# An MLP that changes from its first matrix to its second one token group at a time, with sums of squares added on GpSimd

## The chip, the cores and the metric

The kernel runs on one core of a Trainium2 chip. The metric is the device time of one execution in microseconds (us); several executions are timed, and their median counts. Beside them one execution is profiled: the profile shows what each engine did in it. TensorE is called PE in the profile, VectorE DVE, ScalarE ACT, GpSimd POOL and SyncE, which issues the DMAs, SP.

## The reference

Two layers of a streaming encoder for 1056 tokens (a prompt of 1024 and 32 new ones) and a model width of 1024. Layer 0 mixes tokens with forgetting attention, layer 1 with a gated linear recurrence. The change touches what follows each mixer:

```python
x = x + rmsnorm(out, post_mix_norm[layer])
h = rmsnorm(x, pre_ffn_norm[layer])
u = jax.nn.relu(h @ ffn_w_up[layer])                       # 1024 -> 4096
x = x + rmsnorm((u * u) @ ffn_w_down[layer], post_ffn_norm[layer])   # 4096 -> 1024

def rmsnorm(x, g):
    y = xf * lax.rsqrt(jnp.mean(xf * xf, axis=-1, keepdims=True) + EPS)
    return y * g
```

All of it is float32. A norm needs the sum of squares over the 1024 features of a token before any of its results can be used.

## The kernel before

**Layout.** Features lie on the 128 partitions, tokens along the free axis. The tokens are cut into 4 quarters of 264 (`G`); quarters 0 and 2 are group `c = 0`, quarters 1 and 3 group `c = 1`, and a group's two quarters are its halves `h`. A vector operation on one block of 128 features of a group has 128x528 elements.

**Matmuls.** A float32 operand is written as the sum of two rounded parts, hi and lo, and a product is three matmuls (hi·hi, lo·hi, hi·lo). Making the two parts of a weight block is a *cut* (`cut`: ACT writes hi at L397, DVE subtracts it at L398 for lo), of activations a *split* (`split`, L316 and L317). `unit` multiplies a block of weights (256 columns, up to 4 pairs of 128 rows each) with the activations by seven block products instead of eight. For it the activations of a group are stored as seven *forms* (the four blocks and three combinations of them), and the weights need combinations too, which POOL adds into `Sx` (L336). Each product needs one cut, so a unit has seven cuts and four POOL combinations. With `cs = (0, 1)` a unit uses each cut weight for both groups, with `cs = (0,)` for one. `unit8` does the same block with eight plain products for one group and needs only forms 0, 1, 2 and 4.

**The MLP in `tail`.** `up(i)` computes 256 hidden columns (i = 0 to 15), squares their ReLU, and writes their seven forms to DRAM (`uf`, by `put_u`): a *set*. `down(s)` adds up to four sets into one of four column blocks of the result, so its s runs from 0 to 18 and its first and last units have 1, 2 or 3 pairs. `get_forms(p, c)` reads set p of group c back in parts (264 KB or 132 KB each) through the staging tile `st`, which has four slots, and splits each part into one of four `F` tiles per group. These same `F` tiles hold the operand of the up matrix until its last unit is through with them. Group 0 goes through units 14 to 18 first (`down`), then group 1 (`down8`), so that the norm of group 0 runs beside the matmuls of group 1. The weights come by `load` into two buffers in turn.

**The norms.** `postnorm` runs over eight feature blocks of a group. DVE multiplies y by gain and factor (L276), adds it to x (L279); ACT squares x into `st` (L251), and DVE adds that to a running sum (L252, in `square`). After the eighth block PE adds the sums across partitions by a matmul with ones (`sums`, tile `cs`, L219); from it `rsqrt` makes the factor `rr` of the next norm. `postnorm` runs three times in each layer's `tail` with squares or without: for group 0 and for group 1 after the mixer (kind 1), and for both groups after the MLP (kind 3), the latter with squares in layer 0 alone. `next_h` makes the normed operand of layer 1 from layer 0's result: its sum, then eight products (L789), eight hi parts on ACT (L791) and eight lo parts on DVE (L792).

**Order.** The engines' queues are in order. A scheduler places the instructions; code under `soon()` gets precedence, `behind` and `pin` fix where a PE instruction stands. The PE queue waits at each `cs` matmul until the sum is complete.

Of the kernel before, what the change touches and what calls it, by code (L numbers as in the profile page):

```python
# [26 lines left out]
LAG = 14  # L27
# [38 lines left out]
class K:  # L66
    def __init__(self, ctx, tc, io):
# [9 lines left out]
        self.table = self.pinned = None  # L77
# [185 lines left out]
    def postnorm(self, c, y, x, fr, kind, layer, more=True, hs=(0, 1), tmp=None):  # L263
        sl = slice(hs[0], hs[-1] + 1)
        last = None

        def put(ins):
            nonlocal last
            if last is not None and ins is not None:
                self.behind(ins, last)  # L270
            last = ins or last

        todo = {}
        for j in range(NJ + 2):
            if j < NJ:
                put(self.v.scalar_tensor_tensor(out=y[:, j, sl], in0=y[:, j, sl], scalar=self.gcol(kind, layer, j),  # L276
                                                in1=fr[:, sl], op0=ALU.mult, op1=ALU.mult))
            if 1 <= j <= NJ:
                put(self.v.tensor_tensor(x[:, j - 1, sl], x[:, j - 1, sl], y[:, j - 1, sl], op=ALU.add))  # L279
                if more:  # L280
                    todo[j - 1] = self.square(c, x[:, j - 1, sl], j - 1, hs, tmp)
            if j >= 2 and more:
                put(todo[j - 2](self.v))
# [87 lines left out]
    def unit8(self, c, raw, pairs, evac):  # L371
        nk = len(pairs)
        F = self.F[c]
        for m, (x, z) in enumerate((("A", "B"), ("E", "B"))):
            x, z = self.bank(x), self.bank(z)
            for e, (f, g) in enumerate(((0, 1), (2, 4))):
# [10 lines left out]
                if e == 1:  # L387
                    with self.soon():
                        evac(m, e, 1, z)

# [124 lines left out]
    def tail(self, w_out, layer, sc=None):  # L515
# [5 lines left out]
        with ExitStack() as ctx:  # L521
# [9 lines left out]
            def raws(ring):  # L531
# [4 lines left out]
                def load(src):  # L536
                    n[0] += 1
                    r = rw[n[0] % 2][:, 0:src.shape[1], 0:src.shape[2]]
# [137 lines left out]
            for i in range(NA, 16):  # L676
# [8 lines left out]
            def get_forms(p, c, n=4):  # L685
                for a, b in ((0, 2), (2, 4), (4, 6), (6, 7)):
# [65 lines left out]

            nsq, self.nl = [0, 0], 0
            for s in range(LAG):
                for p in range(4) if s == 0 else (s,) if s > 3 else ():
                    for c in range(2):
                        get_forms(p, c)
                down(s, (0, 1), load)
            get_forms(LAG, 1)
            for s in range(LAG, 19):  # L760
                if s < 16:
                    get_forms(s, 0)
                down(s, (0,), load)
# [17 lines left out]
            def next_h(c, late):  # L781
# [5 lines left out]
                for j in range(NJ):  # L787
# [4 lines left out]
                    self.v.tensor_tensor(hl[:, j], y, hh[:, j].bitcast(F32), op=ALU.subtract)  # L792
# [3 lines left out]
            get_forms(15, 1, 2)  # L796
# [5 lines left out]
            else:  # L802
                next_h(0, self.last_mm)
            for s in range(16, 19):
                down8(s, 1, load2)
# [814 lines left out]
```

## Time and profile before

| | |
|---|---|
| median of 3 runs | 3016.42 us (3013.67 to 3016.75) |
| the profiled execution | 3009.45 us, its span 3007.7 us |
| PE busy | 2845.7 us, 95% of the span |
| DVE busy | 2053.5 us, 68% |
| ACT busy | 1472.0 us, 49% |
| POOL busy | 1468.6 us, 49% |
| mean granted PE clock | 0.972 |
| DMA | 349.36 MB, mean 116 GB/s |

Times inside the profile count from the start of the span. PE is busy nearly throughout; a change of the time must come from the stretches in which it waits or runs at a lower clock, or must make new ones.

### The profile page before, as it was taken

How to read it: one execution, taken by the hardware profiler on the slowest of the kernel's cores; microseconds unless marked ns; L12 is line 12 of the kernel's file. 1: busy time of each engine (PE TensorE's matmuls, PEld its weight loads, DVE VectorE, ACT ScalarE, POOL GpSimd, SP SyncE). 2: the span in 40 equal slices, each digit the busy share in tenths (PEclk: the TensorE clock that was granted, in tenths of full speed). 3: DMA queues.
4: the chain of work that ended last, by engine and by line, in shares of the span. 5: the costliest groups of instructions: out<-in, count | busy, mean ns of one | idle time of the engine just before them, and what ended most of it. 6: DMA issues, size and time to landing. Idle time of an engine off the chain costs nothing.

```text
span 3007.7 us, 56032 instructions
## 1 busy us (share of the span) xinstructions
PE 2845.7 (95%) x21377; PEld 2725.1 (91%) x21377; DVE 2053.5 (68%) x3419; ACT 1472.0 (49%) x3104; POOL 1468.6 (49%) x1595
## 2 busy tenths in 40 slices
PE   7999999999889998999979999999988999899987
PEld 6888888899889998999869999999988999799986
DVE  6788888864785545678888655546488554667787
ACT  6455555555455655544454232322345665644443
POOL 2344444431227775466723644544314886556660
PEclk9999999999989999999989999999999999899997
DMA  5111211144434445445353211115444443544452
GB/s 163 47 48 46 55 46 48 52 113 142 137 129 173 158 145 183 153 132 152 111 161 118 57 56 40 48 33 150 145 126 161 154 166 144 192 143 135 148 166 76
DMA packets 329172, 349.36 MB, mean 116 GB/s; under 512 B 19535, under 2 KB 287703, under 8 KB 328903
## 3 DMA queue, kind: packets, MB, share of 16 engines
q1 hardware_dynamic: 327879, 345.65, 36.6%
q8 instruction: 168, 2.75, 0.4%
q14 instruction: 101, 0.83, 0.1%
q0 software_dynamic: 1024, 0.13, 0.0%
HBM read 238.78 MB, written 106.88 MB: 115 GB/s over the span
## 4 chain that ended last, share of the span: by engine, by line
PE 70%; DVE 13%; DMA 5%; ACT 4%; issue 4%; POOL 4%; SPq 0%; DVEq 0%; ACTq 0%; POOLq 0%
PE mA L410 14%; PE mB L410 11%; PE hj L184 8%; PE pj L184 8%; PE mE L410 5%; PE gp L184 4%; PE po L184 4%; DMA st<-uf 2%; DVE S L398 2%; PE mD L410 1%; DVE F L317 1%; PE lv L1465 1%; POOL hs L310 1%; PE pv L1129 1%; PE ss L1002 1%
## 5 line engine op out<-in xcount | busy, mean ns | idle before, releaser
L410 PE MATMUL mA<-F,S 128*128 128x264 f32 x4404 | 604.8, 289 | 50.3 <-ACT F L316 15.5
L410 PEld LDWEIGHTS mA<-F,S 128*128 128x128 f32 x4404 | 566.0, 191 | 62.8 <-ACT F L316 17.2
L410 PE MATMUL mB<-F,S 128*128 128x264 f32 x4248 | 585.5, 287 | 11.1 <-DVE S L398 4.8
L410 PEld LDWEIGHTS mB<-F,S 128*128 128x128 f32 x4248 | 548.4, 191 | 17.5 <-DVE S L398 9.0
L398 DVE TENSOR_TENSOR S<-Sx,S 128x512 fp32r<-128x512 f32 (+3 forms) x280 | 247.6, 889 | 157.3 <-ACT S L397 155.0
L398 DVE TENSOR_TENSOR S<-raw,S 128x512 fp32r<-128x512 f32 (+3 forms) x282 | 240.4, 857 | 89.6 <-ACT S L397 89.5
L317 DVE TENSOR_TENSOR F<-st,F 128x528 fp32r<-128x528 f32 (+2 forms) x260 | 229.1, 885 | 100.0 <-ACT F L316 99.3
L316 ACT CAST F<-st 128x528 fp32r<-128x528 f32 (+2 forms) x260 | 153.6, 596 | 252.4 <-DMA st<-uf 238.6
L410 PE MATMUL mE<-F,S 128*128 128x264 f32 x1740 | 246.4, 289 | 17.9 <-DVE S L398 9.3
L184 PE MATMUL pj<-H,wh 128*128 128x352 f32 x1152 | 256.7, 341 | 2.1 <-POOL wh L163 1.5
L336 POOL TENSOR_TENSOR Sx<-raw 128x512 f32<-128x512 f32 (+3 forms) x140 | 187.9, 1345 | 132.1 <-DVE S L398 129.6
L410 PEld LDWEIGHTS mE<-F,S 128*128 128x128 f32 x1740 | 225.3, 190 | 26.2 <-DVE S L398 14.5
L310 POOL TENSOR_TENSOR hs<-hs 128x264 f32<-128x264 f32 x216 | 188.4, 891 | 103.5 <-ACT hs L549 101.0
L184 PE MATMUL hj<-h,wh 128*128 128x264 f32 x1600 | 228.7, 289 | 0.0
L170 POOL TENSOR_SCALAR wh<-wr 128x1024 fp32r<-128x1024 f32 x58 | 69.0, 1190 | 319.2 <-PE hj L184 100.2
L184 PEld LDWEIGHTS pj<-H,wh 128*128 128x128 f32 x1152 | 199.8, 192 | 19.0 <-POOL wh L163 1.7
L200 POOL TENSOR_TENSOR e<-e,Y 128x264 f32<-128x264 f32 x170 | 164.0, 974 | 102.1 <-ACT e L741 87.3
L171 DVE TENSOR_TENSOR wl<-wr,wh 128x1024 fp32r<-128x1024 f32 x102 | 135.3, 1328 | 111.1 <-POOL wh L170 59.4
L184 PEld LDWEIGHTS hj<-h,wh 128*128 128x128 f32 x1600 | 206.1, 189 | 1.6
L397 ACT CAST S<-Sx 128x512 fp32r<-128x512 f32 (+3 forms) x280 | 163.6, 585 | 51.3 <-PE mE L410 22.1
L397 ACT CAST S<-raw 128x512 fp32r<-128x512 f32 (+3 forms) x282 | 161.3, 574 | 45.4 <-PE mB L410 32.5
L1125 DVE TENSOR_TENSOR pl<-pf,ph 128x512 fp32r<-128x512 f32 x192 | 127.6, 669 | 54.2 <-POOL ph L1124 29.7
(351 smaller groups left out, 5879.0 us busy)
## 6 DMA issues: line engine op xcount, KB each, us to landing
st<-uf SPq DMA_DIRECT2D x192, 264.0 KB
uf<-hs SPq DMA_DIRECT2D x54, 924.0 KB
raw<-in_ffn_w_up_dram SPq DMA_DIRECT2D x40, 1024.0 KB
raw<-in_ffn_w_down_dram SPq DMA_DIRECT2D x30, 1024.0 KB
wr<-in_hgrn_w_in_dram SPq DMA_DIRECT2D x39, 512.0 KB
wr<-in_fox_w_in_dram SPq DMA_DIRECT2D x32, 512.0 KB
uf<-us SPq DMA_DIRECT2D x10, 924.0 KB
st<-uf SPq DMA_DIRECT2D x64, 132.0 KB
```

The source lines that it names most:

```text
L170: self.g.tensor_scalar(out=wh, in0=raw, scalar1=1.0, scalar2=0.0, op0=ALU.mult, op1=ALU.add)
L171: self.v.tensor_tensor(wl, raw, wh.bitcast(F32), op=ALU.subtract)
L184: ins = self.nc.tensor.matmul(ps, lhsT=ws[kk][a], rhs=xs[kk][b], start=i == 0, stop=i == tot - 1)
L200: self.g.tensor_tensor(out, a, b, op=op)
L310: ins = e.tensor_tensor(f[:, o], f[:, a], f[:, b], op=ALU.subtract)
L316: self.s.copy(hi, src)
L317: self.v.tensor_tensor(lo, src, hi.bitcast(F32), op=ALU.subtract)
L336: self.g.tensor_tensor(src, a, b, op=op)
L397: self.s.copy(hi, src)
L398: self.v.tensor_tensor(lo, src, hi.bitcast(F32), op=ALU.subtract)
L410: ins = self.nc.tensor.matmul(o, lhsT=a[:, i], rhs=F[kp % 4][:, b, f], start=start and n == 0, stop=stop and n == tot - 1, skip_group_chec ...
L1125: self.v.tensor_tensor(pl[:, :N], pf[:, :N], ph[:, :N].bitcast(F32), op=ALU.subtract)
```

## The change

Five edits, in both layers unless said otherwise:

1. The adds of squares in `postnorm` go to GpSimd (`self.g`) instead of DVE, and are no longer chained into DVE's order.
2. The last up unit and the first four down units are done for one group at a time. Up 15 runs for group 0, then for group 1; down 0, 1 and 2 follow for group 0, and the rest alternate. Five more units are cut and combined, and five more weight blocks are loaded.
3. Sets 14 and 15 of group 1, which only `unit8` uses, are read as forms 0, 1, 2 and 4: three parts of 2, 1 and 1 forms instead of four parts of 2, 2, 2 and 1.
4. The weights of down unit 18 (2 of 8 rows) go into the upper half of the buffer that holds those of unit 17 (4 of 8 rows).
5. In layer 0 `next_h(0)` is called after the first half of `down8(16)` instead of ahead of it, and its odd lo parts are subtracted on GpSimd.

```diff
@@ postnorm
             if j >= 2 and more:
-                put(todo[j - 2](self.v))
+                todo[j - 2](self.g)
@@ unit8
                 if e == 1:
                     with self.soon():
                         evac(m, e, 1, z)
+                    if m == 0 and self.mid:
+                        f, self.mid = self.mid, None
+                        f(self.last_mm)
@@ raws
-                def load(src):
-                    n[0] += 1
-                    r = rw[n[0] % 2][:, 0:src.shape[1], 0:src.shape[2]]
+                def load(src, at=0):
+                    n[0] += at == 0
+                    r = rw[n[0] % 2][:, at:at + src.shape[1], 0:src.shape[2]]
@@ tail
-            for i in range(NA, 16):
+            for i in range(NA, 15):
...
-            def get_forms(p, c, n=4):
-                for a, b in ((0, 2), (2, 4), (4, 6), (6, 7)):
+            def get_forms(p, c, n=4, parts=((0, 2), (2, 4), (4, 6), (6, 7))):
+                for a, b in parts:
...
-            for s in range(LAG):
-                for p in range(4) if s == 0 else (s,) if s > 3 else ():
-                    for c in range(2):
-                        get_forms(p, c)
+            up(15, (0,), (hst[2],))
+            get_forms(0, 0)
+            get_forms(1, 0)
+            up(15, (1,), (hst[3],))
+            get_forms(2, 0)
+            down(0, (0,), load)
+            get_forms(3, 0)
+            for p in range(4):
+                get_forms(p, 1)
+            for c, s in ((0, 1), (0, 2), (1, 0), (0, 3), (1, 1), (1, 2), (1, 3)):
+                down(s, (c,), load)
+            for s in range(4, LAG):
+                for c in range(2):
+                    get_forms(s, c)
                 down(s, (0, 1), load)
-            get_forms(LAG, 1)
+            few = ((0, 2), (2, 3), (4, 5))
+            get_forms(LAG, 1, parts=few)
             for s in range(LAG, 19):
                 if s < 16:
                     get_forms(s, 0)
-                down(s, (0,), load)
+                down(s, (0,), load if s < 18 else lambda src: load(src, 4))
...
-                    self.v.tensor_tensor(hl[:, j], y, hh[:, j].bitcast(F32), op=ALU.subtract)
+                    (self.g if j % 2 else self.v).tensor_tensor(hl[:, j], y, hh[:, j].bitcast(F32), op=ALU.subtract)
...
-            get_forms(15, 1, 2)
+            get_forms(15, 1, 2, few)
...
             else:
-                next_h(0, self.last_mm)
+                self.mid = lambda late: next_h(0, late)
             for s in range(16, 19):
-                down8(s, 1, load2)
+                down8(s, 1, load2 if s < 18 else lambda src: load2(src, 4))
```

What the edits move on DVE is seen at two places, and on PE at a third. The first is DVE's queue in layer 0's `postnorm` of group 0 after the attention (`ya` is the mixer's result, `xa` the residual, `wl` the lo part of a weight block of the output projection that PE works on meanwhile). Before, with the adds of squares `st` in line:

```order
L279 TENSOR_TENSOR xa_867_8886<-xa_867_8886,ya_866_8885 128x528
L252 TENSOR_TENSOR st_8881<-st_8881 128x528
L276 SCALAR_TENSOR_TENSOR ya_866_8885<-ya_866_8885,gain,rr_9430 128x528
L279 TENSOR_TENSOR xa_867_8886<-xa_867_8886,ya_866_8885 128x528
L171 TENSOR_TENSOR wl_9663<-wr_9660,wh_9662 128x1024
L252 TENSOR_TENSOR st_8881<-st_8881 128x528
L276 SCALAR_TENSOR_TENSOR ya_866_8885<-ya_866_8885,gain,rr_9430 128x528
```

The same place in the changed program:

```order
L279 TENSOR_TENSOR xa_867_8886<-xa_867_8886,ya_866_8885 128x528
L276 SCALAR_TENSOR_TENSOR ya_866_8885<-ya_866_8885,gain,rr_9430 128x528
L171 TENSOR_TENSOR wl_9663<-wr_9660,wh_9662 128x1024
L279 TENSOR_TENSOR xa_867_8886<-xa_867_8886,ya_866_8885 128x528
L276 SCALAR_TENSOR_TENSOR ya_866_8885<-ya_866_8885,gain,rr_9430 128x528
L279 TENSOR_TENSOR xa_867_8886<-xa_867_8886,ya_866_8885 128x528 x2
```

All seven adds of this `postnorm` are gone from DVE's queue; the other rows keep their order but for one `wl`, which moves ahead of an `xa` add.

The second place is DVE's queue at the start of the down matrix in layer 0 (`F` the splits of sets read back, `S` the cuts, whose size tells the unit: 128x128 is down 0, 128x256 down 1; `Y` the result). Before:

```order
L317 TENSOR_TENSOR F_919_9752<-st_8881,F_919_9752 128x528
L724 TENSOR_TENSOR Y_1200_13956<-mB_14071,e_14101 128x264
L398 TENSOR_TENSOR S_9964<-Sx_9965,S_9964 128x128
L317 TENSOR_TENSOR F_920_9761<-st_8881,F_920_9761 128x528
L398 TENSOR_TENSOR S_9964<-raw_934_9962,S_9964 128x256
L317 TENSOR_TENSOR F_919_9752<-st_8881,F_919_9752 128x264
L317 TENSOR_TENSOR F_978_10693<-st_8881,F_978_10693 128x528
L317 TENSOR_TENSOR F_977_10684<-st_8881,F_977_10684 128x528
```

In the changed program, down 0 of group 0 and the first cuts of down 1:

```order
L401 TENSOR_TENSOR S_9964<-Sx_9965,S_9964 128x128 x2
L401 TENSOR_TENSOR S_9964<-raw_934_9962,S_9964 128x128
L728 TENSOR_TENSOR Y_1184_13719<-mB_14025,e_14044 128x264
L401 TENSOR_TENSOR S_9964<-Sx_9965,S_9964 128x128
L317 TENSOR_TENSOR F_921_9770<-st_8881,F_921_9770 128x528
L401 TENSOR_TENSOR S_9964<-raw_935_9963,S_9964 128x256 x2
L317 TENSOR_TENSOR F_976_10675<-st_8881,F_976_10675 128x528
L728 TENSOR_TENSOR Y_1184_13719<-mB_14063,e_14058 128x264
```

Before, splits of both groups (`F_918` to `F_921` are group 0, `F_976` to `F_979` group 1) stand between few cuts; in the changed program each unit of one group brings its own seven cuts, and from the first cut of up 15 to the first cut of down 4 there are 70 cuts instead of 35, with the same splits.

The third place is PE's queue at the sum of squares that `next_h(0)` needs in layer 0 (`cs`; `mA`, `mE` are result banks). Before:

```order
L410 MATMUL mE_18075<-F_978_10693,S_9964 128x264
L410 MATMUL mE_18075<-F_979_10702,S_9964 128x264
L219 MATMUL cs_17983<-st_8881,ones 128x264
L219 MATMUL cs_17991<-st_8881,ones 128x264
L410 MATMUL mA_18026<-F_977_10684,S_9964 128x264
```

In the changed program:

```order
L413 MATMUL mA_18214<-F_978_10693,S_9964 128x264
L413 MATMUL mA_18214<-F_979_10702,S_9964 128x264
L219 MATMUL cs_18122<-st_8881,ones 128x264
L219 MATMUL cs_18130<-st_8881,ones 128x264
L413 MATMUL mE_18164<-F_977_10684,S_9964 128x264
```

Between the sum ahead of it (for the norm after the MLP) and this one PE has 117 matmuls before and 138 in the changed program.

## Rows read from the trace of the kernel before

**Rows 1.** The page's busy time of each engine (us, share, instructions).
```profile
PE 2845.7 (95%) x21377; PEld 2725.1 (91%) x21377; DVE 2053.5 (68%) x3419; ACT 1472.0 (49%) x3104; POOL 1468.6 (49%) x1595
```

**Rows 2.** Timeline of PE: sums that it waited for; idle time in brackets.
```profile
799.51 1.16 PE L219 MATMUL cs<-st,ones 128*128 128x264 f32 x4 [1.35 <-DVE st L252]
868.25 2.12 PE L219 MATMUL cs<-st,ones 128*128 128x264 f32 x4 [5.58 <-DVE st L252]
1553.36 2.13 PE L219 MATMUL cs<-st,ones 128*128 128x264 f32 x4 [6.78 <-DVE st L252]
1611.82 1.75 PE L219 MATMUL cs<-st,ones 128*128 128x264 f32 x4 [3.29 <-DVE st L252]
2210.67 2.13 PE L219 MATMUL cs<-st,ones 128*128 128x264 f32 x4 [3.51 <-DVE st L252]
2279.65 2.13 PE L219 MATMUL cs<-st,ones 128*128 128x264 f32 x4 [8.01 <-DVE st L252]
```

**Rows 3.** Timeline of PE in layer 0's change of matrix.
```profile
1164.14 3.09 PE L410 MATMUL mA<-F,S 128*128 128x264 f32 x24
1203.11 1.03 PE L410 MATMUL mA<-F,S 128*128 128x264 f32 x3 [7.48 <-ACT Y L712]
1236.40 3.10 PE L410 MATMUL mA<-F,S 128*128 128x264 f32 x24
```

**Rows 4.** Busy time by stretch: PE, PEld, DVE, ACT, POOL; clock, DMA share, GB/s.
```profile
779.00:800.00 21.00, 19.65 (x162) 19.40 (x161) 20.31 (x28) 9.59 (x18) 3.90 (x2) 1.00 0.45 142
849.00:869.00 20.00, 14.42 (x113) 13.97 (x112) 19.16 (x30) 10.93 (x22) 2.46 (x4) 0.89 0.54 187
1164.00:1257.00 93.00, 78.68 (x592) 76.09 (x591) 62.26 (x103) 53.53 (x125) 41.96 (x45) 0.91 0.57 186
1462.00:1500.00 38.00, 32.96 (x239) 30.90 (x237) 34.52 (x45) 19.55 (x42) 29.40 (x26) 0.96 0.25 77
1526.00:1554.00 28.00, 17.14 (x123) 15.99 (x122) 26.02 (x46) 14.30 (x27) 1.55 (x2) 0.82 0.27 89
1554.00:1586.00 32.00, 24.84 (x165) 22.63 (x164) 28.34 (x52) 17.14 (x36) 8.48 (x8) 0.93 0.28 78
```

**Rows 5.** Timeline of DVE in layer 0's first postnorm: start, duration.
```profile
784.52 0.70 DVE L279 TENSOR_TENSOR xa<-xa,ya 128x528 f32<-128x528 f32 x1
785.13 0.70 DVE L252 TENSOR_TENSOR st<-st 128x528 f32<-128x528 f32 x1
785.75 0.76 DVE L276 SCALAR_TENSOR_TENSOR ya<-ya,gain,rr 128x528 f32<-128x528 f32 x1
```

**Rows 6.** Timeline of POOL just after it: adds of other squares.
```profile
801.09 2.75 POOL L252 TENSOR_TENSOR st<-st 128x528 f32<-128x528 f32 x2 [6.66 <-ACT st L251]
805.90 1.39 POOL L252 TENSOR_TENSOR st<-st 128x528 f32<-128x528 f32 x1 [2.05 <-DVE st L252]
```

**Rows 7.** Timeline of DVE beside those adds.
```profile
802.09 0.43 DVE L209 SCALAR_TENSOR_TENSOR rt<-cs,rr 128x264 f32<-128x264 f32 x1 [0.91 <-ACT rr L207]
802.56 1.57 DVE L210 SCALAR_TENSOR_TENSOR rt<-rt,rr 128x264 f32<-128x264 f32 x1
804.16 0.44 DVE L211 SCALAR_TENSOR_TENSOR rr<-rt,rr 128x264 f32<-128x264 f32 x1
806.13 1.45 DVE L211 SCALAR_TENSOR_TENSOR rr<-rt,rr 128x264 f32<-128x264 f32 x1
```

**Rows 8.** Timeline of DVE in the change of matrix: cuts and a split, undisturbed.
```profile
1173.84 0.69 DVE L398 TENSOR_TENSOR S<-Sx,S 128x512 fp32r<-128x512 f32 x1 [0.28 <-ACT S L397]
1181.05 0.71 DVE L317 TENSOR_TENSOR F<-st,F 128x528 fp32r<-128x528 f32 x1
1188.52 0.28 DVE L398 TENSOR_TENSOR S<-raw,S 128x128 fp32r<-128x128 f32 x1
1227.83 0.43 DVE L317 TENSOR_TENSOR F<-st,F 128x264 fp32r<-128x264 f32 x1 [2.51 <-ACT F L316]
```

**Rows 9.** POOL's combinations from 1164 to 1257: count, busy us, mean ns.
```profile
L336 POOL TENSOR_TENSOR Sx<-raw 128x512 f32<-128x512 f32 x4 | 5.5, 1379 | 7.9 <-DVE S L398 7.9
L336 POOL TENSOR_TENSOR Sx<-raw 128x384 f32<-128x384 f32 x2 | 2.0, 1016 | 5.5 <-DVE S L398 5.5
L336 POOL TENSOR_TENSOR Sx<-raw 128x128 f32<-128x128 f32 x2 | 1.0, 480 | 0.6 <-DVE S L398 0.6
```

More of the change, by code (lines that the diff above doesn't have):

```diff
@@ L76, in __init__ @@
         self.pp = self.pool("pp", 1, PSUM)
-        self.table = self.pinned = None
+        self.table = self.pinned = self.mid = None
         nc.scalar.preload_act_table_set(TABLE)
```

## The prediction

> **What bounds the kernel now.** I read the page's busy times first. PE is busy for 95% of the span and DVE for 68% [rows 1], so on the average nothing but PE counts. Then I read the timeline of PE for its idle time, because only that can be won, and DVE's for what ends it. Two of the places where PE waits are touched by the change. The first are the sums across partitions: PE waits there for 1.35, 5.58, 6.78, 3.29, 3.51 and 8.01 us, each time for DVE's last add of squares [rows 2]. The second is the change of matrix. In layer 0 up 15 begins at 1164.14 [rows 3]. It has 168 matmuls and down 0 to 2 have 252; PE at full clock needs 0.121 us for one (162 in 19.65 us, in the first stretch of rows 4), so down 3 could begin 51 us later, at 1215. It begins at 1236.40 [rows 3], so 21 us go there; the longest single wait is 7.48 us, for a copy that ACT makes into the result `Y`. The table by stretch then tells what sets the pace beside these waits: DVE is busy for 20.31 of 21 us and 19.16 of 20 us ahead of the first two sums, for 26.02 of 28 and 28.34 of 32 ahead of the next two [rows 4]. The share of 68% hides that in the norms DVE is the bound. In the change of matrix it isn't full: 62.26 of 93 us.
>
> **Squares on GpSimd.** 42 adds leave DVE: seven in each of six `postnorm`s that sum squares. On DVE an add takes 0.61 to 0.62 us from its start to the next one's (784.52, 785.13, 785.75) [rows 5]. On POOL the same operation takes 1.38 us (two in 2.75, one in 1.39) [rows 6]; I use 1.3 for the part in which it works. What an add on POOL does to DVE is read from DVE's operations beside those adds. One that takes 0.43 us by itself took 1.57, and the next of the kind 1.45 [rows 7]; the first ends at 804.13, where POOL's pair ends at 803.84, the second at 807.58, where POOL's ends at 807.29 [rows 6, 7]. So each was held until POOL was through, and lost 1.14 and 1.02 us. An add that moves thus frees 0.62 us of DVE and costs it about 1.03 us (the lower of the two, rounded, since an operation that comes late in the add is held for less). On an engine that is full, seven of them are 7 x 0.41 = 2.9 us. To this comes the last add, which nothing hides: 1.3 us instead of 0.70, +0.6. That makes +3.5 us for a sum that PE waits for. The bounds: if POOL doesn't hold DVE at all, -7 x 0.62 + 0.6 = -3.7; if every add costs DVE its whole 1.3, 7 x 0.68 + 0.6 = +5.4. Four of the sums, both after the mixers of the two layers (799.51, 868.25, 2210.67, 2279.65 [rows 2]), have nothing else that changes: 4 x 3.5 = **+14 us**. The Trainium skill ("SBUF — State Buffer", section "Who interferes with whom") says that a DVE instruction with two SBUF inputs contends with a GpSimd instruction that reads SBUF, and that whoever issues first holds the shared port pair for the whole instruction while the other blocks fully. By that rule, the trace agrees (+1.14 and +1.02, each released 0.29 us after POOL's end), but taken to the letter each add would cost its whole length, and the four sums would give 22 us instead of 14.
>
> **Layer 0 behind the MLP.** The two other sums have 7 adds each, and now four lo parts per group on POOL besides. For group 0 (1526 to 1586) that is 11 x 0.41 = 4.5, with the tail 5.1; DVE has 5.6 us free there (2.0 of 28 and 3.7 of 32 [rows 4]), of which I let 2 take some of it up: +3. For group 1 it is 3.5 and a part of the lo parts: +4. Moving `next_h(0)` behind half a `down8` lays 21 more matmuls, 2.6 us, ahead of PE's wait for its sum. What was waited for there, though, is DVE [rows 2], which has the same work to do, and these matmuls are missing behind the wait; I put it at nothing; bounds are -2.6 and +2.6. Together **+7 us**.
>
> **The change of matrix.** What goes: PE no longer needs both groups' sets for down 0, and group 1's `Y` is written later, so the 7.48 us for `Y` should go. What comes, per layer: 35 cuts, seven for each of five units (one of 512 columns, twice; 128, 256 and 384 wide ones for down 0 to 2 and the like), 20 combinations, five weight blocks. A cut's time on DVE is its duration less some 0.08 us, by which neighbours overlap: 0.61 for 512 columns, 0.20 for 128 [rows 8], 0.34 and 0.47 in line between them. Counted as one more up 15 and downs 0, 1, 2 and 3 (3 is as wide as 15), it is 7 x (2 x 0.61 + 0.47 + 0.34 + 0.20) = 15.6 us of DVE. The combinations take 1.38 us of POOL at 512 columns, 1.02 at 384, 0.48 at 128 [rows 9], about 0.75 in between: 4 x (2 x 1.38 + 1.02 + 0.75 + 0.48) = 20 us of POOL. If they held DVE as the adds did, they would cost it 1.03/1.3 = 0.8 us for each of theirs; where DVE has gaps, nothing. I take the middle, 0.45, so 9 us. DVE then has 62.3 + 15.6 + 9 = 87 us of work where before all took 93. A stretch of this kernel in which units of one group run with their own cuts is 1462 to 1500: there DVE gets to 34.52 of 38 us, 0.91 [rows 4]. 87/0.91 = 95 us instead of 93, **+2 us** for a layer. What is late next is then the lo part of the next unit and the split of the next set, which queue behind each other on DVE, in front of every unit of one group; PE's granted clock was 0.91 in this stretch already [rows 4], so waits by pieces don't restore it. Bounds: PE's own need is 588 x 0.121 = 71 us, and with a wait or two for cuts some 80, -13; with 0.8 instead of 0.45, DVE has 94 us and the stretch takes 103, +10. The five loads of at most 1 MB go beside a DMA share of 0.57 [rows 4] and are put at nothing, at the latest a part of these bounds. For both layers **+4 us**.
>
> **The rest.** Sets 14 and 15 of group 1 in three parts with four forms: on DVE three splits of 528 and one of 264 columns (3 x 0.63 + 0.34 = 2.23 us) become one and two (1.31) [rows 8], 0.92 less for each of four sets; DVE is nearly full there, so I take **-3 us**, bounds 0 and -3.7. Two weight blocks in one buffer let the last load start earlier; no wait of PE in rows 2 and 3 ends on such a load, and the work of units 16 and 17 hides it: nothing. If that cover were missing, it would be part of a wait of one load, under 2 us.
>
> **Sum.** 14 + 7 + 4 - 3 = **+22 us**. The profiled execution took 3009.45 us, its span 3007.7; with +22 that is 3031.5. The median of the runs is 3016.42, 7 us above the profiled one, and the same sum on it gives **3038 us**.
>
> **The rivals.** *Slower by more*: POOL's combinations hold DVE as its adds do, all through the change of matrix, so that each layer loses 10 instead of 2 us. That is +38, 3054 us. For it speaks that the only pieces where both engines met show 0.8 [rows 6, 7]; against it, that DVE has gaps there and POOL's work can fall into them. Chance 0.14. *Faster, by the change of matrix*: it is the largest loss that the change touches, 21 us per layer [rows 3], and if one group's units start early enough, PE runs at near its pace: 80 us instead of 93, -26 in both layers instead of +4. Then the sum is 22 - 4 - 26 = -8, 3008 us. It decides from about 81 us downward: the rest of the sum is 18 us, which 9 us per layer make even, and 12 us per layer turn into over 0.2%. Against it stands DVE's 62 us, which grow by 16 at the least. Chance 0.14. *Faster, by the squares*: POOL doesn't hold DVE when the queue is full, because DVE's operations follow each other closely and POOL gets its turn only in gaps. Then the four sums give 4 x -3.7 = -15 and the two behind the MLP -7 instead of +7: -15 - 7 + 4 - 3 = -21, 2995 us. What was held in rows 6 and 7 speaks against it. Chance 0.10. *No change*: adds at half that price (+7 for six), the change of matrix at -2 per layer, -3 for the parts: 0, 3016 us. Chance 0.16.
>
> **The numbers.** The forecast, 3023 to 3048 by its bounds, has 0.46. A measurement of this kernel tells no change from one within 0.2%, 6 us: 3010.4 to 3022.4. Faster are the two rivals that end below it, 0.24; the same 0.16; slower 0.46 + 0.14 = 0.60. The range leaves out about 0.1 at each end, the squares that cost nothing and the top of the dearest case: 3002 to 3052.
>
> **What the profile of the changed kernel would show.** POOL has 62 adds of squares instead of 20, at 1.3 us or more. `postnorm`'s products and adds on DVE, 0.70 and 0.76 us before [rows 5], are stretched to 1.5 and more beside them; PE's waits for the first two and the last two sums grow by about 3.5 us each, to 5, 9, 7 and 11.5, and are ended by POOL. From up 15 to down 4 it takes about 95 us, DVE is busy for over 0.9 of it, and no wait of 7 us for `Y` is left, but many of 1 to 3 us for cuts and splits. I am wrong about the squares if those rows of DVE keep their length; about the change of matrix if DVE's busy time there stays under 80 us or PE's idle time shrinks to a few us.

## The result: slower by 1.6%, and the profile after

The changed kernel takes 3062.53 us (median of 4 runs, 3061.66 to 3065.17) against 3015.05 before on the same chip: ratio 1.0161, interval 1.0143 to 1.0179, or +47 us. The sign was forecast, the size (+22) was half of it. Its profiled execution has a span of 3060.1 us, 52.4 more than before.

The page's busy times of the changed kernel, as in rows 1:

```profile
PE 2873.9 (94%) x21377; PEld 2745.4 (90%) x21377; DVE 2107.7 (69%) x3435; ACT 1504.1 (49%) x3170; POOL 1599.7 (52%) x1685
```

DVE has only 16 instructions more than before and is busy for 54 us more: many of its instructions became longer, as the rows below show. PE's sums, which answer to rows 2:

```profile
802.95 1.16 PE L219 MATMUL cs<-st,ones 128*128 128x264 f32 x4 [3.27 <-POOL st L252]
873.37 2.13 PE L219 MATMUL cs<-st,ones 128*128 128x264 f32 x4 [3.17 <-POOL st L252]
1572.83 2.13 PE L219 MATMUL cs<-st,ones 128*128 128x264 f32 x4 [1.97 <-POOL st L252]
1634.28 2.13 PE L219 MATMUL cs<-st,ones 128*128 128x264 f32 x4 [7.64 <-POOL st L252]
2241.63 2.13 PE L219 MATMUL cs<-st,ones 128*128 128x264 f32 x4 [4.91 <-POOL st L252]
2316.87 2.13 PE L219 MATMUL cs<-st,ones 128*128 128x264 f32 x4 [5.23 <-POOL st L252]
```

All are now ended by POOL. The last wait alone misleads (5.58 became 3.17 at the second): PE also waits ahead of it for the cuts that DVE makes late. So I compare the starts of the sums. The table gives how much longer each stretch between them took than before, in the changed kernel and in runs told below (e1 squares alone, e2 switch alone, e3 the other edits, e13 changed kernel with lo parts on DVE, e14 changed kernel with less on POOL, e15 kernel before with less on POOL). Ahead of 774, where no edit is, these traces differ from the one before by -3.4 to +3.6 us, so that a difference of one to three us in a long stretch means little by itself.

| stretch (time before) | after | e1 | e2 | e3 | e13 | e14 | e15 |
|---|---|---|---|---|---|---|---|
| 774 to 799.5, first norm | +3.5 | +3.5 | 0 | 0 | +3.5 | 0 | 0 |
| to 868, second norm | +1.7 | +2.4 | -0.1 | +0.6 | +2.9 | +0.3 | +0.4 |
| to 1526, MLP of layer 0 | +11.1 | +2.1 | +9.0 | -1.5 | +11.4 | -1.3 | -7.4 |
| to 1612, norms behind it | +6.3 | +6.1 | -2.7 | -0.5 | +2.6 | -2.6 | 0 |
| to 2095, mixer of layer 1 | +6.5 | +0.6 | -1.2 | +7.6 | -0.5 | +0.4 | -1.2 |
| to 2280, its two norms | +8.2 | +9.2 | +0.6 | +0.4 | +9.0 | -0.2 | +1.2 |
| to 2934, MLP of layer 1 | +16.5 | +5.1 | +16.3 | +8.1 | +15.3 | +5.8 | -5.7 |
| to the end | -1.3 | +0.4 | -0.4 | -1.3 | -1.8 | -1.6 | +0.1 |

**Inside the first norm**, DVE (first) and POOL (second) of the changed kernel, timeline:

```profile
784.46 0.71 DVE L279 TENSOR_TENSOR xa<-xa,ya 128x528 f32<-128x528 f32 x1
785.08 1.84 DVE L276 SCALAR_TENSOR_TENSOR ya<-ya,gain,rr 128x528 f32<-128x528 f32 x1
786.84 1.54 DVE L279 TENSOR_TENSOR xa<-xa,ya 128x528 f32<-128x528 f32 x1
788.31 1.83 DVE L276 SCALAR_TENSOR_TENSOR ya<-ya,gain,rr 128x528 f32<-128x528 f32 x1
790.06 1.83 DVE L279 TENSOR_TENSOR xa<-xa,ya 128x528 f32<-128x528 f32 x1
...
783.50 2.85 POOL L252 TENSOR_TENSOR st<-st 128x528 f32<-128x528 f32 x1 [8.18 <-DVE ya L276]
787.80 3.52 POOL L252 TENSOR_TENSOR st<-st 128x528 f32<-128x528 f32 x2
```

All but the first of these adds and products of DVE, 0.70 and 0.76 us in rows 5, take 1.5 to 1.8, and POOL's first add takes 2.85 where one alone took 1.39 [rows 6]: each engine waits for the other.

**The change of matrix**, the stretch from PE's first matmul of up 15 to its first of down 4 in layer 0 and in layer 1 of the changed kernel, as in rows 4 (PE, PEld, DVE, ACT, POOL; clock, DMA), with layer 1 before as the third row, and PE's longest waits in layer 0:

```profile
1173.02:1276.71 103.69, 88.46 (x591) 82.15 (x590) 93.58 (x138) 69.39 (x162) 68.57 (x64) 0.90 0.57 186
2615.71:2718.47 102.76, 85.52 (x590) 77.95 (x589) 95.00 (x138) 69.33 (x162) 68.38 (x64) 0.95 0.59 187
2574.90:2666.69 91.79, 77.80 (x591) 74.69 (x589) 61.77 (x102) 53.59 (x125) 42.31 (x45) 0.91 0.59 186
```
```profile
1188.46 1.24 PE L413 MATMUL mE<-F,S 128*128 128x264 f32 x8 [1.90 <-DVE S L401]
1197.54 4.77 PE L413 MATMUL mB<-F,S 128*128 128x264 f32 x20 [2.83 <-DVE S L401]
1211.68 0.75 PE L413 MATMUL mA<-F,S 128*128 128x264 f32 x4 [1.79 <-DVE S L401]
```

The 7.48 us for `Y` are gone [rows 3], and waits for cuts stand in their place. The stretch takes 103.7 us instead of 92.7, and 102.8 instead of 91.8 in layer 1. DVE is busy for 0.90 and 0.92 of it, about the share that the prediction took, but with 93.6 and 95.0 us of work and not 87. PE's idle time in layer 0 hardly grew (103.7 less 88.5 is 15.2; before, 93.0 less 78.7 was 14.3 [rows 4]); its busy time did, by 10 us for the same 590 matmuls, mostly because more of them run at the lower of its two clock levels. The second wait above shows it: behind it 20 matmuls take 4.77 us, 0.24 each, where the prediction read 0.121 at full clock, and the granted clock over them is 0.50, which is 1.2 GHz:

```profile
1197.54:1202.31 4.77, 4.77 (x21) 4.77 (x22) 4.38 (x8) 2.44 (x6) 1.64 (x2) 0.50 0.81 273
```

In the whole stretch some 100 matmuls start 0.18 to 0.26 us after the one ahead of them; before, 35 did.

**A wait that the prediction had not.** PE, ACT and POOL of the changed kernel in the MLP's first units, layer 0 and layer 1; the last two rows are of the kernel before, PE in layer 0 and POOL in layer 1:

```profile
917.42 2.13 PE L413 MATMUL mA<-F,S 128*128 128x264 f32 x8 [6.27 <-ACT F L316]
2360.13 2.13 PE L413 MATMUL mA<-F,S 128*128 128x264 f32 x8 [5.08 <-ACT F L316]
```
```profile
915.64 1.73 ACT L316 CAST F<-st 128x1848 fp32r<-128x1848 f32 x1 [7.81 <-DMA uf<-us]
2358.35 1.73 ACT L316 CAST F<-st 128x1848 fp32r<-128x1848 f32 x1 [5.55 <-DMA uf<-us]
```
```profile
901.59 4.58 POOL L336 TENSOR_TENSOR Sx<-raw 128x512 f32<-128x512 f32 x1 [5.04 <-DMA raw<-in_ffn_w_up_dram]
906.13 2.13 POOL L310 TENSOR_TENSOR us<-us 128x264 f32<-128x264 f32 x2
2343.90 4.93 POOL L336 TENSOR_TENSOR Sx<-raw 128x512 f32<-128x512 f32 x1 [5.37 <-DMA raw<-in_ffn_w_up_dram]
2350.49 3.65 POOL L310 TENSOR_TENSOR us<-us 128x264 f32<-128x264 f32 x4
```
```profile
910.28 1.24 PE L410 MATMUL mA<-F,S 128*128 128x264 f32 x8 [2.10 <-ACT F L316]
2305.91 1.85 POOL L336 TENSOR_TENSOR Sx<-raw 128x512 f32<-128x512 f32 x1 [2.50 <-DMA raw<-in_ffn_w_up_dram]
```

The last tile of group 1's operand (tag `f3`) lies in the memory of hidden set 3, and may be written only when that set has gone to DRAM. Its forms (`us`) stand on POOL behind a combination that waits for a weight load and then takes 4.6 and 4.9 us. No edit touches this place, but the scheduler places its instructions anew in every kernel. In layer 0 the long wait goes with the squares: it is 6.26 or 6.27 us in e1, e13 and the changed kernel, which have them on POOL, and 2.1 before and in e2, e3, e4 and e14, which have them on DVE. In layer 1 it was no wait of PE before, and it is 4.5 to 5.1 in each of e1 to e4. Among the runs below that keep POOL's combinations there and don't hold its order by hand, every wait of over 4 us has a first combination of 3.7 to 4.9 us, and wherever the first combination took 1.3 to 1.9 the wait is under 2.5. So POOL's own work, held beside DVE's, is in the chain; that this alone makes the tile late was not tested.

### The profile page after: what moved, and what is told of

Its sections match the earlier page's. It is cut to its first block, busy times and chain, and to the rows that moved or that the text cites. A ratio compares the mean times of both kernels' runs of the same rounds, so it can differ in the third digit from the quotient of the medians.

```text
span 3060.1 us, 56334 instructions
## 1 busy us (share of the span) xinstructions
PE 2873.9 (94%) x21377; PEld 2745.4 (90%) x21377; DVE 2107.7 (69%) x3435; ACT 1504.1 (49%) x3170; POOL 1599.7 (52%) x1685
## 4 chain that ended last, share of the span: by engine, by line
PE 42%; DVE 10%; issue 2%; POOL 2%; ACT 2%; DMA 2%; DVEq 0%; ACTq 0%; POOLq 0%; SPq 0%
PE mA L413 10%; PE mB L413 9%; PE hj L184 9%; PE mE L413 4%; DVE S L401 3%; PE gp L184 2%; PE po L184 2%; PE lv L1481 1%; PE mD L413 1%; DVE F L317 1%; DMA st<-uf 1%; DVE Y L276 1%; POOL Sx L336 1%; PE lv L1496 1%; DVE xs L279 1%
## 5 line engine op out<-in xcount | busy, mean ns | idle before, releaser
L413 PE MATMUL mA<-F,S 128*128 128x264 f32 x4404 | 618.6, 290 | 68.3 <-ACT F L316 26.5
L413 PE MATMUL mB<-F,S 128*128 128x264 f32 x4332 | 615.4, 291 | 21.5 <-DVE S L401 16.3
L413 PEld LDWEIGHTS mB<-F,S 128*128 128x128 f32 x4332 | 571.4, 194 | 31.3 <-DVE S L401 22.5
L401 DVE TENSOR_TENSOR S<-Sx,S 128x512 fp32r<-128x512 f32 (+3 forms) x320 | 271.5, 853 | 168.1 <-ACT S L400 164.8
L401 DVE TENSOR_TENSOR S<-raw,S 128x512 fp32r<-128x512 f32 (+3 forms) x312 | 270.0, 870 | 98.6 <-ACT S L400 98.6
L336 POOL TENSOR_TENSOR Sx<-raw 128x512 f32<-128x512 f32 (+3 forms) x160 | 219.8, 1377 | 128.3 <-DVE S L401 115.4
L400 ACT CAST S<-Sx 128x512 fp32r<-128x512 f32 (+3 forms) x320 | 183.5, 574 | 71.8 <-POOL Sx L336 30.5
L400 ACT CAST S<-raw 128x512 fp32r<-128x512 f32 (+3 forms) x312 | 175.3, 566 | 61.3 <-PE mB L413 52.5
L252 POOL TENSOR_TENSOR st<-st 128x528 f32<-128x528 f32 x62 | 110.0, 1775 | 126.6 <-ACT st L251 113.1
```

The lines of the kernel that those rows point to most:

```text
L252: return lambda eng: eng.tensor_tensor(acc, acc, t, op=ALU.add)
L336: self.g.tensor_tensor(src, a, b, op=op)
L400: self.s.copy(hi, src)
L401: self.v.tensor_tensor(lo, src, hi.bitcast(F32), op=ALU.subtract)
L413: ins = self.nc.tensor.matmul(o, lhsT=a[:, i], rhs=F[kp % 4][:, b, f], start=start and n == 0, stop=stop and n == tot - 1, skip_group_chec ...
```

## Experiments

Each run has its own median beside the kernel before on the same chip.

**e1, squares alone.** The one line of edit 1 put into the kernel before.

> The kernel before with the adds of squares on GpSimd and nothing else. The theory (an add on POOL holds DVE, which is full in the norms, and what is lost shows at the sums and behind them): PE's time between the landmarks of the two traces grew by some 2, 7, 15 and 12 us around the sums of the changed kernel, of which the 15 behind the first MLP also hold edit 5; so +25 to +32 us, about 3043. The prediction's own price (3.5 us for each of six sums) gives +21. The rival that the squares cost nothing and the loss is the change of matrix alone gives 0 or less.

3040.45 us, ratio 1.0099 (1.0084 to 1.0114), +29. The theory's size. Stretches with sums give 3.5 + 2.4 + 6.1 + 9.2 = 21, the MLPs 7, with waits for the tile `f3` of 6.26 us in layer 0 (2.10 before) and 4.86 in layer 1.

**e2, the switch alone.** Edit 2 put into the kernel before.

> The kernel before with the switch to one group at a time between the MLP's matrices and nothing else. The theory: DVE's work there grows to 93 us (as read in the changed kernel) and the stretch takes 102 instead of 93 us, so +8 us in each layer, +16, about 3031. The prediction's price was +4 in all. If the loss there came only through what the other edits leave behind, it is 0.

3033.14 us, 1.0075 (1.0058 to 1.0092), +22: 9.0 in layer 0; 16.3 in layer 1, of which 5.08 are the wait for `f3`. The stretch of the change of matrix itself grew by 9.5 and 12.1.

**e3, edits 3 to 5 alone.**

> The kernel before with edits 3 to 5 (fewer parts for the last sets, two weight blocks in a buffer, the sum of the next layer's norm later with four of its lo parts on GpSimd), without the squares and without the switch. The traces show 3 to 5 us won in the first layer between the down units and the norm behind them, and a loss behind it that cannot be told from that of the squares. Theory: -3 for the parts and +3 for the lo parts on POOL, so 0, between -5 and +5, 3010 to 3020. If the later sum costs by itself what the stretch lost, +8.

3022.05 us, 1.0039 (1.0024 to 1.0054), +11, outside what was expected: 7.6 behind the MLP's norms, 8.1 in layer 1's MLP, of which 5.07 are the `f3` wait.

**e4, the changed kernel with the squares on DVE.**

> The changed kernel with the adds of squares on DVE again. By the theory it loses the whole cost of the squares: -25 to -32 us against the changed kernel, so 3031 to 3038, +16 to +22 against the kernel before. By the rival that the change of matrix is all of the loss it stays at 3062.

3044.12 us, 1.0108 (1.0093 to 1.0123), +33. On top of the other edits the squares cost 16 (1.0161 less 1.0108), not 25 to 32. Single edits add up to more (62) than the whole (47); 10 of these 15 us are the `f3` wait of layer 1, some 5 us that the sum counts three times and the whole has once.

**e5, POOL's order held.** In `unit`, for the first unit of both groups, the combinations are put behind the forms `us` (an excerpt; `last_us` is the last form operation, set in `up8` and cleared at the end of `unit`):

```python
ins = self.g.tensor_tensor(src, a, b, op=op)
if self.last_us: self.behind(ins, self.last_us)
```

> The changed kernel, with the four combinations of the first up unit of both groups held behind the four additions on POOL that make the forms of the last set of the group ahead of it. In the changed kernel and in the first four runs POOL's queue has them the other way round, and PE waits 5.1 us (layer 1) and 6.3 us (layer 0) for the last split of the operand of group 1, which shares its memory with that set. Theory: these waits are a by-product of the order that the scheduler chose, and not of the squares; with the order restored PE's waits there fall to under 1 us and the kernel is 9 to 11 us shorter than the changed one, about 3052. Rival: they come from the late factor of group 1's norm, and the order changes nothing: 3062.

3055.27 us, 1.0163 (1.0147 to 1.0178): by ratio no better than the changed kernel. In layer 0 no wait for the tile is left, but two for cuts, 3.1 us together; in layer 1 the wait for it fell from 5.08 to 3.63. The two MLP stretches fell by about 3 us each. So the order is a part of it at most; why the tile comes late is not settled by this run.

**e6, edits 3 to 5 with that order and all lo parts on DVE.**

> The third run (edits 3 to 5 alone, 11 us slower than before) with the same order restored and with all lo parts of the next layer's operand on DVE again, so that of edit 5 only the later call is left. The third run lost 7.6 us between the second sum behind the first MLP and the next sum, and 5.5 to 8 us in the second layer's MLP. Theory: the first is the lo parts on POOL, the second the order; without both it is -2 to -4 against the kernel before, about 3008. Rival: the later call of the sum costs the 7.6 us: +8.

3009.09 us, 1.0008 (0.9999 to 1.0017), no change. The stretch from 1612 to 2095 is back to +0.2. The parts win nothing that shows.

**e7 and e9, does POOL's reading hold DVE?** The kernel before with that order, and in `postnorm`, beside DVE's own add, an operation on the dead square: e7 the first line, e9 the second.

```python
self.g.tensor_tensor(t, t, t, op=ALU.add)
self.g.memset(t, 0.0)
```

> The kernel before (with that order of POOL held) and seven additions on POOL in each postnorm that sums squares: each adds a square to itself in its own place after DVE has used it, so nothing waits for its result but the next square in that place. DVE keeps its own seven adds. Theory (an addition on POOL holds DVE): each costs DVE 1.0 to 1.3 us, so each of the waits at the six sums grows by 5 to 9 us and the kernel by 30 to 50 us, about 3050. Rival (DVE is not held; the squares cost only because POOL's last adds end late): the waits stay and it is +0 to +5.

> The control to the run with seven additions beside DVE's own in each postnorm (+39 us): the same places, the same waits, but POOL fills the dead square with zeros instead of adding it to itself, so it reads nothing. Theory (what holds DVE is POOL's reading of operands in the same memory): the waits at the sums stay as before, and it is +0 to +6 (the order of the forms in layer 1 may still cost some 4). Rival (any POOL instruction there holds DVE, or the places come free too late): +20 or more.

e7: 3046.08 us, 1.0129 (1.0114 to 1.0144), +39. e9: 3008.88 us, 1.0012 (1.0003 to 1.0022), +2. The first two sums of e7, then of e9, and POOL's groups of the added operations (busy, mean ns):

```profile
804.52 2.13 PE L219 MATMUL cs<-st,ones 128*128 128x264 f32 x4 [6.63 <-DVE st L252]
879.90 2.13 PE L219 MATMUL cs<-st,ones 128*128 128x264 f32 x4 [6.71 <-DVE st L252]
L286 POOL TENSOR_TENSOR st<-st 128x528 f32<-128x528 f32 x42 | 65.1, 1553 | 58.0 <-DVE st L252 58.0
```
```profile
795.34 1.16 PE L219 MATMUL cs<-st,ones 128*128 128x264 f32 x4 [1.39 <-DVE st L252]
864.01 2.13 PE L219 MATMUL cs<-st,ones 128*128 128x264 f32 x4 [5.61 <-DVE st L252]
L286 POOL MEMSET st<- 128x528 f32 x42 | 22.4, 538 | 58.3 <-DVE st L252 56.0 <-ACT S L403 2.0
```

Only ACT's next square in the same place waits for these results, and DVE does not idle for it: in the six norms of e7 it is idle for 1.2 us together between its first product and its last addition to x. So the 39 us come from longer operations of DVE: 0.92 for each of 42 additions. The writes are a third as long and cost a sixteenth. The Trainium skill ("SBUF — State Buffer", section "Who interferes with whom") says that a DVE instruction with two SBUF inputs contends with a GpSimd instruction that reads SBUF, not with one that only writes it; the two runs agree.

**e8, the switch without combinations.** In `unit`, with that order, `if b is not None and len(cs) == 2`: units of one group cut the weights themselves, which leaves out a part of the product. This takes in 20 units per layer, not the 10 that the expectation speaks of: up 0 to 4 of group 1 and down 14 to 18 of group 0 too.

> The second run (the switch alone, 22 us slower than before), with that order held, and without the 40 combinations on POOL of the ten extra or split units of each layer: their cuts read the weights instead, which leaves out part of the product. DVE keeps all cuts. Theory (POOL's combinations hold DVE): without them DVE has some 78 us of work in the stretch, which takes 85 to 90 us; the kernel is at -2 to -12 against before, about 3005. Rival (the 35 cuts alone are too many for DVE and ACT, or the splits come too late): the stretch stays at 100 us, and it is at +12 to +17 (the switch less the order).

2977.41 us, 0.9906 (0.9889 to 0.9923), -30, below the range; a part of it is won in the other ten units (in layer 0 the stretch of down 14 to 18 of group 0 is 10 us shorter). **e11** keeps all combinations, with that order, those of the same 20 units on DVE: `(self.g if len(cs) == 2 else self.v).tensor_tensor(src, a, b, op=op)`.

> The second run (the switch alone, +22) with the 40 combinations of the units of one group on DVE instead of POOL, and the order of POOL's form additions held. Each costs DVE 0.2 to 0.61 us, 18 us per layer; without any combination the stretch took 82 us instead of 100. If what POOL's combinations cost is the time they hold DVE (17 us by DVE's busy time with and without them), DVE is as full as with them and the stretch stays near 98 to 100 us: +12 to +20. If it is their own length in the chain from weights to cut, 88 to 92 us and -4 to +4.

3009.54 us, 1.0015 (1.0002 to 1.0028), +3. The stretch from up 15 to down 4 in layer 0 of e2, e8 and e11, and DVE's cuts of raw weights in it (busy, mean ns) before and in e2, e8 and e11:

```profile
1165.52:1267.72 102.20, 85.07 (x591) 77.79 (x589) 94.79 (x138) 69.40 (x162) 68.68 (x64) 0.95 0.59 188
1162.36:1247.14 84.78, 80.11 (x590) 74.89 (x589) 72.74 (x138) 68.86 (x162) 26.07 (x26) 0.98 0.69 227
1169.69:1266.98 97.29, 84.41 (x591) 78.86 (x589) 88.01 (x175) 68.93 (x161) 26.68 (x26) 0.93 0.60 199
```
```profile
L398 DVE TENSOR_TENSOR S<-raw,S 128x512 fp32r<-128x512 f32 x6 | 4.4, 727 | 2.7 <-ACT S L397 2.7
L398 DVE TENSOR_TENSOR S<-raw,S 128x512 fp32r<-128x512 f32 x12 | 15.6, 1298 | 0.2 <-ACT S L397 0.2
L401 DVE TENSOR_TENSOR S<-raw,S 128x512 fp32r<-128x512 f32 x27 | 21.6, 808 | 3.9 <-ACT S L400 3.0 <-PE mE L413 0.8
L401 DVE TENSOR_TENSOR S<-raw,S 128x512 fp32r<-128x512 f32 x12 | 9.0, 747 | 0.3 <-ACT S L400 0.3
```

POOL's 43 us of combinations keep DVE busy for 22 us (94.8 against 72.7): a cut that takes 0.73 us before takes 1.30 beside them. Done by DVE they take it 15 us (88.0): DVE has less to do when it does POOL's work as well. The stretch of e11 is 97.3 us (97.7 in layer 1): 5 and 6 shorter than in e2 (102.2 and 103.9; the 82 and 100 of the expectation were read at other places of the queue), but 4.6 and 5.9 longer than before. So about half of what the switch loses there is the combinations' place on POOL; the other half stays when DVE does them, and falls away, with more, when they are left out (e8: 8.0 and 2.8 shorter than before). That e11's time is yet only 3 us above the kernel before comes from the other ten units, whose combinations it moved too; by themselves these win 11 us (e15). Against e15 the switch still costs 14 us (1.0015 against 0.9968).

**e10, the switch by eight products.** The ten units of the switch by `up8` and `down8`: no combinations, fewer cuts, 84 matmuls more per layer. **e12** is the changed kernel with this, squares and lo parts on DVE.

> The kernel before with the switch to one group at a time, but with the ten units of one group done by eight plain products (unit8) instead of seven: no combinations on POOL, four cuts instead of seven for each, 84 matmuls more per layer (10 us of PE). Theory (the switch loses by POOL's combinations and DVE's cuts, not by its order): DVE has about 60 us of work in the stretch and PE 82 us, so the stretch takes 84 to 88 us instead of 93, and the kernel is at -10 to -18, about 2995. Rival (the splits of the sets read back come too late in any case): 93 us and more, +0 to +10.

> The changed kernel with the squares and the lo parts on DVE and the units of one group by eight products; the switch, the fewer parts, the shared buffer and the later sum are left. If the switch with eight products wins 10 to 18 and the rest is worth 0 to -4, 2990 to 2997 us, -10 to -20 against the kernel before.

3006.56 us, 1.0005 (0.9993 to 1.0017), and 3009.3 us, 1.0018 (1.0006 to 1.0030). PE's waits over 0.5 us there fall from 12 to 4 us, and the 10 us of added matmuls take that up. Expected gains missed.

**e13, the changed kernel with all lo parts on DVE; e14, with squares, lo parts and combinations of one-group units on DVE.**

> The changed kernel (+48) with the four lo parts in each of the two calls of the next layer's operand on DVE again, and nothing else. Theory: their POOL work (1.3 us or more each, beside DVE's other four, each pair in a chain) is what the stretch from the second sum behind the first MLP to the next layer's first sum lost, 6.5 us in the changed kernel and 7.6 in the third run: about -6 against the changed kernel, +42 against the one before. Rival: it was the later call: +48, no change.

> The changed kernel with all that it puts on POOL taken by DVE: the adds of squares, the lo parts, and the combinations of all units of one group (in this run as in the two with combinations changed these are 20 units per layer: the ten of the switch, five up units of group 1 and the last five down units of group 0). What is left is the switch, the fewer parts, the shared buffer and the later sum. Theory (the loss is POOL's work, which costs DVE more than if DVE did it): -2 to +4 against the kernel before. Rival (cuts and order of the switch cost by themselves): +10 to +20.

e13: 3049.82 us, 1.0141 (1.0126 to 1.0156); the stretch to 2095 falls from +6.5 to -0.5, as forecast, and the later sum, which e13 keeps, costs nothing. What they did in the changed kernel (POOL, DVE, PE):

```profile
1645.68 3.21 POOL L808 TENSOR_TENSOR h<-xs,h 128x528 fp32r<-128x528 f32 x2 [0.27 <-ACT h L807]
1650.74 1.81 DVE L808 TENSOR_TENSOR h<-xs,h 128x528 fp32r<-128x528 f32 x1
1652.47 2.32 DVE L171 TENSOR_TENSOR wl<-wr,wh 128x1024 fp32r<-128x1024 f32 x1
1654.85 2.13 PE L184 MATMUL hj<-h,wl 128*128 128x264 f32 x8 [1.78 <-DVE wl L171]
```

e14: 3010.23 us, 1.0010 (1.0000 to 1.0020), 0.10% instead of 1.61%. But like e11 it also moves the combinations of ten units per layer that the change leaves alone. The run to hold against it is the kernel before with those on DVE, e15 below: 2996.43 us on the same chip, 14 us less. So with nothing more on POOL about 14 us of the loss of 47 are left, and 33 go with the engine. In the traces (e14 less e15) they show as 4.6 and 6.1 us in the two stretches of the change of matrix, which take 95.9 and 97.3 us in e14, and as 4.64 of the `f3` wait in layer 1, which e15 doesn't have.

**e15 to e18: the theory turned on the kernel before.** e15 puts the combinations of its one-group units on DVE (the line of e11), e16 also the projections' adds of squares, e17 all combinations, e18 also the subtractions of `put_u`.

> The kernel before with the combinations of its ten units of one group per layer (five up, five down) on DVE instead of POOL. Theory: each takes DVE 0.2 to 0.61 us instead of holding it 0.4 to 1.4; where those units are, PE waits in sum 4 to 5 us per layer for cuts and splits, of which it can win half: -2 to -6. Rival (DVE is full there and gets more work): +2 to +6.

> The run before this one and, with it, the adds of squares of the projections on DVE too (before, six of eight per group are on POOL; two of them were seen to hold the factor's steps on DVE by 1.0 and 1.1 us). Theory: the factor of each mixer norm comes 1 to 2 us earlier at four sums: -4 to -8 against that run, if PE waits for it. Rival (DVE is full and these adds now stand in its queue): 0 to +6.

> The run before this (squares of the projections and combinations of one-group units on DVE, -16) with the combinations of the units of both groups on DVE too: no combination is left on POOL. In those units DVE is busy for some 60 to 70% and PE hardly waits, so there is little to win: 0 to -3 against that run. Rival: DVE becomes full there, +5.

> The run with all combinations on DVE, and the four subtractions that make the forms of each hidden set on DVE as well (0.42 us each on DVE, 0.9 on POOL as read in the kernel before). They hold DVE less than the long combinations did, and they feed a DMA that others wait for late only at two places. Theory: the last split of the operand of group 1 waits less, 0 to -5 against the run with all combinations; rival: 128 more operations of 0.34 us on DVE come ahead of cuts where it is full, +5.

| run | us | ratio to before | interval |
|---|---|---|---|
| e15 | 2996.43 | 0.9968 | 0.9956 to 0.9981 |
| e16 | 2991.66 | 0.9948 | 0.9933 to 0.9963 |
| e17 | 2988.44 | 0.9938 | 0.9913 to 0.9962 |
| e18 | 2980.09 | 0.9895 | 0.9877 to 0.9914 |

e15 and e18 won more than expected, e16 and e17 what was. The busy times of e18, the fastest:

```profile
PE 2826.8 (95%) x21377; PEld 2715.2 (91%) x21377; DVE 2167.5 (73%) x3975; ACT 1491.3 (50%) x3104; POOL 805.5 (27%) x1039
```

POOL gave up 663 us and DVE took on 114 [rows 1]. The group of e18 in which DVE cuts raw weights (busy, mean ns) shows from where:

```profile
L398 DVE TENSOR_TENSOR S<-raw,S 128x512 fp32r<-128x512 f32 (+3 forms) x282 | 186.7, 664 | 80.2 <-ACT S L397 79.0
```

The same 282 cuts took 240.4 us, 857 ns each, in the kernel before. The wait for `f3` in layer 1 is 0.31 us in e18, 6.26 in e16.

## Why the prediction was wrong in size

- **Squares on GpSimd: right in mechanism, and near in price at the sums.** Six sums were priced at 14 + 7 = 21 us with lo parts; the stretches around them give 3.5 + 1.7 + 6.3 + 8.2 = 19.7. The 1.03 us by which an addition holds DVE came out as 0.92 (e7). PE's last waits were not read rightly: 5, 9, 7 and 11.5 us were foretold for the first two and the last two sums, 3.3, 3.2, 4.9 and 5.2 came, since PE also waits ahead of them. The rivals that POOL doesn't hold DVE, or at half price, fell.
- **Lo parts on POOL: the step "a part of the lo parts" failed.** They were priced inside the sums' stretches alone. With them on DVE (e13) those behind the MLP are 3.7 us shorter, and the stretch behind them is 7.0 us shorter, where the lo parts hold the weight cuts of the next mixer's matmuls; nothing was put there. (By the runs' ratios the two together are 0.20%, 6 us.)
- **The change of matrix: the term was mis-sized, +2 per layer against 11.** The share of about 0.91 held; DVE's added work did not. It was put at 25 us, 16 for the cuts and 9 for the combinations, and is 31 (93.6 less 62.3). The combinations were taken to hold DVE for 0.45 of POOL's time (said to be the middle of nothing and 0.8, which is 0.4); by e8 it is 0.52 (22 of 43 us). POOL's work grew by 27 us (68.6 less 41.7) and not 20, since DVE holds POOL as well. By these numbers some 14 of the 31 are the combinations, an estimate, and 17 the cuts. The rival of +10 per layer named 94 us of DVE and 103 for the stretch, and that came; its reason, a hold of 0.8, did not, so its number is in part luck. The combinations are most of the loss: all 40 of a stretch cost 17.4 us in layer 0 and 14.9 in layer 1 (e2 less e8), so the 20 added ones some 8 of the 9.5 and 12.1 us of e2, an estimate; e8 has all the added cuts and is shorter than the kernel before. Their place on POOL is about half of the loss (e2 against e11); the other half stays when DVE does them.
- **No term: the wait for `f3`.** 6.3 us in layer 0 (2.1 before) and 5.1 in layer 1 of the changed kernel. It was not looked for, since no edit is near; the scheduler's new order was there to be read. In layer 0 it goes with the squares (e1, e13). In layer 1 it comes and goes: e10 and e14 have 4.6 us, e16 6.3, e13 none. e5 shows POOL's order to be a part of it at most; what else makes the tile late stays open.
- **Fewer parts: -3 was forecast, and nothing shows** (e6). The later sum and the shared buffer cost nothing, as said.

## What to carry to other kernels

Where VectorE is the bound, look at what GpSimd reads beside it before giving GpSimd more: in this kernel an addition of two 128x528 operands cost VectorE more when GpSimd did it (0.92 to 1.14 us) than when VectorE did (0.62). Busy times show it as the same instructions grown longer; taking work off GpSimd is then worth a run by itself, here 1.05%. A control that moves more than the change did needs its own baseline: e14 looked like the kernel before only because it also moved other work, as e15 shows. And read the scheduler's order of every engine after a change, also where the diff doesn't reach.

## Not expected of the hardware

That moving 663 us of work from GpSimd costs VectorE only 114 us of busy time (e18), and that 42 zero fills of 0.54 us on GpSimd in a full norm cost 2 us where 42 additions cost 39.
